# Layer norm over a matmul on one core: the opening worked on five row tiles with three quarters put aside, instead of seven with one

## The chip, the cores and the metric

The kernel runs on one core of one Trainium2 chip. The metric is the time of one execution on the device in microseconds (us), lower is better. The kernel before takes 249.03 us (median of three runs, 248.82 to 249.81).

The engines are named as in the profile: PE is TensorE, which multiplies and also transposes; PEld is its loading of weights; DVE is VectorE, ACT is ScalarE, POOL is GpSimd, and SP is SyncE, which here only issues DMA transfers. Each engine works through its own instructions in order and waits on semaphores for the others.

## The reference

```
x = np.matmul(a, b)                      # a, b: 2048 x 2048, float32
mean = np.mean(x, axis=-1, keepdims=True)
var = np.var(x, axis=-1, keepdims=True)
normalized = (x - mean) / np.sqrt(var + eps)
return (gamma * normalized + beta).astype(np.float32)
```

A row of the result can only be normalized when all its 2048 columns are there.

## The kernel before

**Tiling.** The rows of `a` form 16 row tiles of 128. The inner dimension forms 16 k tiles of 128, and four of them make a chunk (`KC`). The columns of `b` form four quarters of 512 (`NB`). One accumulator is one quarter of one row tile, 128 x 512 in float32. It fills one of eight PSUM banks and takes 16 matmuls, one per k tile, so there are 16 x 4 x 16 = 1024 matmuls (`mm`, L86). PSUM banks come from one pool of eight (L57), which the transposes use as well.

**Input.** All of `b` is brought to SBUF once, as float16 (`b16`). A piece of it lands in float32 in a staging buffer (the pool `stg` has six, each of 128 x 1024) and DVE casts it. `load_b1` brings one k tile of a quarter (256 KB), `load_b2` two k tiles (512 KB). PE needs `a` transposed. For the row tiles of the opening, `load_a1` and `load_a2` bring pieces of one chunk for one or two row tiles, DVE casts them, PE transposes them in `turn` (four 128 x 128 transposes per row tile and chunk, L239), and ACT copies the result to SBUF (L241). For the other row tiles, POOL issues a DMA that brings and casts a whole row tile (L339), and SP issues a DMA that transposes it (`turn_ahead`, L406). The POOL instruction at L290 copies one column of the last piece of `b`, so that the POOL transfers start only after it.

**The opening.** The first `R` = 7 row tiles are worked on together, because each piece of `b` that lands then feeds seven matmuls per k tile.

1. The first chunk of quarter 0. The pieces of `a` and `b` come in turn (list `arrivals`, L164): a0 b0 a1 b1 a2 b2 a3 b3 a4 a5 a6. PE multiplies what is there; where it would wait, matmuls on zeros are put in (`filler`, L232). The seven part sums over k tiles 0 to 3 are put aside by ACT in the SBUF tiles `x` (L297).
2. Quarter 1 over all 16 k tiles, in the order k tile by k tile, with the transposes of the later chunks in between (L300 to L315).
3. The other 12 k tiles of quarter 0 (L318 to L328). DVE adds what had been put aside (L325) and takes the batch statistics (L327).
4. Quarters 2 and 3 of these row tiles, one row tile after the other, three of them by quarter (`n_first`), the others by row.

Other accumulators are brought to SBUF by ACT and their statistics taken by DVE (`evacuate`, L96 and L97).

**After the opening** each row tile takes its four quarters in turn. `stats` joins the statistics, and `queue_norm` puts two pieces of normalization (two quarters each) into a list, from which `drain` takes one after a quarter; each piece ends in a store by SP. The transfers of the transposed row tile are issued four row tiles ahead (`turn_ahead(i + 4)`, L418). The last row tile has an ending of its own (`finish_row`).

**Order.** There is no scheduler: `manual_schedule` keeps each engine's instructions in the order in which the code emits them. A load function emits its DMA on SP and its cast on DVE, so where `bring` is called in between, the cast stands in DVE's queue at that place. A DMA into a staging buffer waits until DVE has cast what was in it.

Of the kernel before, what the change touches and what calls it, by code (L numbers as in the profile page):

```python
# [16 lines left out]
def kernel(  # L17
# [9 lines left out]
    nc = tc.nc  # L27
# [9 lines left out]
    KC = 4  # L37
    KW = KC * P
    n_kc = n_kt // KC
    R = 7  # L40
    early, e_cap, p_cap = 4, 3, 7
    n_first = 3
    assert n_kt % KC == 0 and n_nb == 4 and R % 2 == 1 and n_mt > R > n_first

    if isinstance(eps, bass.AP):
        eps_ap, eps_val = eps, None
# [36 lines left out]
    def mm(i, q, kt, first, last):  # L83
        if (i, q) not in acc:
            acc[i, q] = bank(f"acc{i}_{q}")
        nc.tensor.matmul(  # L86
            acc[i, q], at(i)[:, kt, :], b16[:, kt, ds(q * NB, NB)],
            start=first, stop=last,
        )
# [95 lines left out]
    def load_a1(i, c):  # L185
        st = half_stage()
        nc.sync.dma_start(st, a[ts(i, P), ts(c, KW)])  # L187
        a16_room(i, c)
        nc.vector.tensor_copy(a16_of[i, c], st)  # L189
# [9 lines left out]
    def load_b1(k):  # L199
        st = half_stage()  # L200
        nc.sync.dma_start(st, b[ts(k, P), 0:NB])  # L201
        nc.vector.tensor_copy(b16[:, k, 0:NB], st)  # L202

    def load_b2(k, q):
        st = stg.tile([P, 2, NB], FP32, tag="st", name=f"stb{q}_{k}")
        nc.sync.dma_start(
            st, b[ds(k * P, 2 * P), ds(q * NB, NB)].rearrange("(t p) n -> p t n", p=P))
        nc.vector.tensor_copy(b16[:, k:k + 2, ds(q * NB, NB)], st)  # L208
        return st
# [3 lines left out]
    def load_pair(j, c):  # L213
        if len(pairs[j]) == 2:
            load_a2(pairs[j][0], c)
        else:
            load_a1(pairs[j][0], c)

    for what in arrivals:
        (load_a1(what[1], 0) if what[0] == "a" else load_b1(what[1]))  # L220
    for c in range(n_kc):
        for h in (0, 1):
            load_b2(c * KC + 2 * h, 1)
            if c + 1 < n_kc:
                load_pair(2 * h, c + 1)
                load_pair(2 * h + 1, c + 1)

    warm = bank("warm")

    def filler(n, to=None):  # L230
        for _ in range(n):
            nc.tensor.matmul(warm if to is None else to, zeros[:, 0:P], zeros, start=True, stop=True)  # L232

    def turn(rows, c):
        n = len(rows)
        t_ps = psum.tile([P, n, KC, P], FP16, tag="ps", name=f"tps{rows[0]}_{c}")
        for m, i in enumerate(rows):
            for j in range(KC):
                nc.tensor.transpose(t_ps[:, m, j, :], a16_of[i, c][:, ts(j, P)], ident)  # L239
# [4 lines left out]
    queue, own = [], []  # L244
    turned, landed = set(), set()

    def emit(n):
        for _ in range(min(n, len(queue))):
            i, kt = queue.pop(0)
            done[i] += 1  # L250
            mm(i, 0, kt, done[i] == 1, done[i] == KC)

    done = [0] * R
    gaps = {0: (9, 3), 1: (1, 2), 2: (1, 2), 3: (3, 1), 4: (3, 0)}
    for what in arrivals:
        if what[0] == "b":
            k = what[1]
            now = [(i, k) for i in sorted(turned)]
            new = {i for i, _ in own}
            queue += [x for x in now if x[0] not in new] + own  # L260
            queue += [x for x in now if x[0] in new]
            own = []
            landed.add(k)
            continue
        i = what[1]
        if i < early:
            queue += own
            own = []
            emit(len(queue))
        before, after = gaps.get(i, (0, 0))  # L270
        filler(before)
        turn([i], 0)
        filler(after)
        if i >= early:
            emit(e_cap)
        queue += own
        turned.add(i)
        own = [(i, k) for k in sorted(landed)]
    queue += own
    queue.sort()  # L280

    later = [(k, 0) for k in range(KC, n_kt, 2)]
    later += [(k, q) for q in range(2, n_nb) for k in range(0, n_kt, 2)]

    def bring(n):
        for _ in range(n):
            k, q = later.pop(0)
            st = load_b2(k, q)
            if not later:
                nc.gpsimd.tensor_copy(gate, st[:, 0, 0:1])  # L290


    for p in range(R):
        emit(KC - done[p])
        xs[p] = xpool.tile([P, N], FP32, tag="x", name=f"x{p}")
        bnst[p] = stat.tile([P, n_nb, 6], FP32, tag="bnst", name=f"bnst{p}")
        nc.scalar.copy(xs[p][:, 0:NB], acc.pop((p, 0)))  # L297


    spots = {(h, p): 2 * h + m for h in (0, 1) for m, p in enumerate((2, 5))}  # L300
# [10 lines left out]
    for p in range(R):  # L311
        for kt in range(n_kt - KC, n_kt):
            mm(p, 1, kt, False, kt == n_kt - 1)
        bring(1)
        evacuate(p, 1)  # L315


    bring(len(later) - 4)  # L318
    for kt in range(KC, n_kt - KC):
        for p in range(R):  # L320
            mm(p, 0, kt, kt == KC, False)
    for p in range(R):
        for kt in range(n_kt - KC, n_kt):
            mm(p, 0, kt, False, kt == n_kt - 1)
        nc.vector.tensor_tensor(  # L325
            xs[p][:, 0:NB], acc[p, 0], xs[p][:, 0:NB], AluOp.add)
        nc.vector.bn_stats(bnst[p][:, 0, :], xs[p][:, 0:NB])  # L327
        bring(min(1, len(later)))  # L328
# [64 lines left out]
    def quarter(i, q):  # L393
        for kt in range(n_kt):
            mm(i, q, kt, kt == 0, kt == n_kt - 1)
# [9 lines left out]
                new_pair(t // 2)  # L405
            nc.sync.dma_start_transpose(at(t), a16[t])  # L406
# [59 lines left out]
```

## Time and profile before

| what | value |
|---|---|
| runs shown | 248.82, 249.03, 249.81 us |
| the profiled execution's own time | 249.5 us |
| its span, first to last instruction | 247.7 us |
| mean granted PE clock over the span | 0.989 |
| PE busy | 240.7 us (97%) |
| DVE busy | 173.0 us (70%) |
| ACT busy | 56.9 us (23%) |
| DMA read and written | 35.67 and 16.78 MB |

The durations below come from the profiled execution. Its own time is 1.8 us more than its span, and 0.5 us more than the median of the runs. In the profile, "L86" is line 86 of the kernel, and an entry such as "acc<-b,at 128x512 x1024" gives what is written and read, its shape and the number of instructions. Busy times of matmuls overlap, so that their mean duration (379 ns for those of L86) is longer than the step from one to the next.

### The profile page before, as it was taken

The numbers are of one execution on the slowest core, as the hardware profiler recorded it, in microseconds if no ns is written. First come the engines' busy times: TensorE is split into PE (matmuls) and PEld (weight loads), VectorE is DVE, ScalarE is ACT, GpSimd is POOL, SyncE is SP. The second block draws the span as 40 slices with busy tenths as digits, with TensorE's granted clock in tenths as the row PEclk, the third lists the DMA queues.
The fourth block names the chain that finished last, engine by engine and source line by source line (L and its number), as shares of the span: only waits on it lengthen the run. The fifth ranks groups of instructions, "written<-read, shape, count | busy, mean of one in ns | idle before, by whom it ended". The sixth has DMA issues, their size and how long they took to land.

```text
span 247.7 us, 3055 instructions
## 1 busy us (share of the span) xinstructions
PE 240.7 (97%) x1175; PEld 110.5 (45%) x1175; DVE 173.0 (70%) x307; ACT 56.9 (23%) x101; POOL 5.6 (2%) x15
## 2 busy tenths in 40 slices
PE   8999999999999999999999999999999999999983
PEld 3445555444444444444444444444444444444430
DVE  1454555965799999999999492856658292947873
ACT  2276446400013312221112121212111121112100
POOL 0000000000030000000000000000000000000000
PEclk9999999999999999999999999999999999999995
DMA  5999999999999239999999979180903122120404
GB/s 147 331 390 385 379 363 389 387 386 385 390 350 210 99 128 221 201 281 252 120 285 324 252 186 266 68 219 3 253 1 125 47 85 85 67 102 3 171 0 169
DMA packets 37846, 52.64 MB, mean 213 GB/s; under 512 B 20292, under 2 KB 20292, under 8 KB 37576
## 3 DMA queue, kind: packets, MB, share of 16 engines
q1 hardware_dynamic: 36536, 47.73, 58.1%
q0 software_dynamic: 1296, 4.72, 12.0%
q8 instruction: 9, 0.15, 0.2%
q14 instruction: 5, 0.04, 0.1%
HBM read 35.67 MB, written 16.78 MB: 212 GB/s over the span
## 4 chain that ended last, share of the span: by engine, by line
PE 92%; DMA 3%; SPq 2%; DVE 1%; issue 0%; ACT 0%
PE acc L86 88%; DMA st<-in_a_dram 3%; PE tps L239 2%; PE w L379 1%; SPq L187 1%; SPq L201 1%; DVE x L389 0%; DVE bnst L363 0%; DVE x L366 0%; DVE a16s L189 0%; PE nm_ps L374 0%; DVE mv L103 0%; ACT lead L375 0%; DVE nm L371 0%; DVE ve L105 0%
## 5 line engine op out<-in xcount | busy, mean ns | idle before, releaser
L86 PE MATMUL acc<-b,at 128*128 128x512 f16 x1024 | 224.1, 379 | 0.0
L86 PEld LDWEIGHTS <-at 128*128 128x128 f16 x1024 | 99.5, 98 | 117.8 <-ACT at L241 1.1
L97 DVE BATCH_NORM_STATS2 bnst<-x 128x6 f32<-128x512 f32 x56 | 38.4, 687 | 36.7 <-ACT x L96 36.7
L96 ACT COPY x<-acc 128x512 f32<-128x512 f32 x56 | 32.7, 585 | 129.5 <-PE acc L86 129.4
L118 DVE SCALAR_TENSOR_TENSOR x<-x,rstd,beta_b 128x512 f32<-128x512 f32 x61 | 43.1, 748 | 0.5
L112 DVE SCALAR_TENSOR_TENSOR x<-x,mv,gamma_b 128x512 f32<-128x512 f32 x60 | 42.1, 744 | 0.0
L208 DVE CAST b<-stb 128x1024 f16<-128x1024 f32 x30 | 20.8, 692 | 14.9 <-DMA stb<-in_b_dram 14.5
L241 ACT COPY at<-tps 128x512 f16<-128x512 f16 (+1 forms) x19 | 15.0, 787 | 21.2 <-PE tps L239 21.2
L232 PE MATMUL warm<-zeros 128*128 128x512 f16 x33 | 11.0, 466 | 1.2 <-DVE zeros L153 1.2
L197 DVE CAST a16s<-sta 128x1024 f16<-128x1024 f32 x9 | 6.2, 694 | 6.1 <-DMA sta<-in_a_dram 6.1
L107 ACT ACTIVATE sq<-ve 128x1 f32<-128x1 f32 x16 | 3.2, 203 | 31.3 <-DVE ve L105 31.3
L239 PEld LDWEIGHTS <-a16s 128*128 128x128 f16 x112 | 7.6, 99 | 6.2 <-DVE a16s L189 2.9
L239 PE MATMUL tps<-ident,a16s 128*128 128x128 f16 x112 | 9.6, 222 | 0.6 <-DVE a16s L189 0.5
L189 DVE CAST a16s<-st 128x512 f16<-128x512 f32 x10 | 4.3, 425 | 6.3 <-DMA st<-in_a_dram 6.3
L339 POOL DMA_DIRECT2D a<-in_a_dram x9 | 4.9, 547 | 70.0 <-DMA at<-a 69.7
L232 PEld LDWEIGHTS <-zeros 128*128 128x128 f16 x33 | 3.5, 114 | 5.3 <-issue 2.4
L327 DVE BATCH_NORM_STATS2 bnst<-x 128x6 f32<-128x512 f32 x7 | 4.9, 695 | 0.2
L325 DVE TENSOR_TENSOR x<-acc,x 128x512 f32<-128x512 f32 x7 | 4.8, 681 | 0.0
L103 DVE BATCH_NORM_AGGREGATE mv<-bnst 128x2 f32<-128x24 f32 x16 | 4.2, 264 | 0.5
L297 ACT COPY x<-acc 128x512 f32<-128x512 f32 x7 | 3.5, 632 | 0.0
L202 DVE CAST b<-st 128x512 f16<-128x512 f32 x4 | 1.7, 428 | 2.3 <-DMA st<-in_b_dram 2.3
L105 DVE TENSOR_TENSOR ve<-mv,eps_t 128x1 f32<-128x1 f32 x16 | 2.6, 160 | 0.5
(26 smaller groups left out, 17.4 us busy)
## 6 DMA issues: line engine op xcount, KB each, us to landing
stb<-in_b_dram SPq DMA_DIRECT2D x30, 512.0 KB, 7.4
out_dram<-x SPq DMA_DIRECT2D x30, 512.0 KB, 3.0
sta<-in_a_dram SPq DMA_DIRECT2D x9, 512.0 KB, 7.5
a<-in_a_dram POOLq DMA_DIRECT2D x9, 512.0 KB, 8.0
st<-in_a_dram SPq DMA_DIRECT2D x10, 256.0 KB, 7.0
st<-in_b_dram SPq DMA_DIRECT2D x4, 256.0 KB, 5.8
gamma_b<-in_gamma_dram SPq DMA_DIRECT2D x1, 1024.0 KB, 9.4
beta_b<-in_beta_dram SPq DMA_DIRECT2D x1, 1024.0 KB, 11.3
```

Of the source, the lines that this page charges most:

```text
L86: nc.tensor.matmul(acc[i, q], at(i)[:, kt, :], b16[:, kt, ds(q * NB, NB)], start=first, stop=last,)
L96: nc.scalar.copy(xs[i][:, qs], acc[i, q])
L97: nc.vector.bn_stats(bnst[i][:, q, :], xs[i][:, qs])
L112: nc.vector.scalar_tensor_tensor(xs[i][:, qs], xs[i][:, qs], mv[:, 0:1], gamma_b[:, qs], AluOp.subtract, AluOp.mult)
L118: nc.vector.scalar_tensor_tensor(xs[i][:, qs], xs[i][:, qs], rstd, beta_b[:, qs], AluOp.mult, AluOp.add)
L197: nc.vector.tensor_copy(held["a"][:, ds(i % KC, 2), :], st)
L208: nc.vector.tensor_copy(b16[:, k:k + 2, ds(q * NB, NB)], st)
L232: nc.tensor.matmul(warm if to is None else to, zeros[:, 0:P], zeros, start=True, stop=True)
L239: nc.tensor.transpose(t_ps[:, m, j, :], a16_of[i, c][:, ts(j, P)], ident)
L241: nc.scalar.copy(pair[i0 // 2][:, ds(i0 % 2, n), ds(c * KC, KC), :], t_ps)
L327: nc.vector.bn_stats(bnst[p][:, 0, :], xs[p][:, 0:NB])
L339: nc.gpsimd.dma_start(a16[i], a[ts(i, P), :])
```

## The change

The opening works on five row tiles (`R` = 5) instead of seven.

- The first chunk's pieces come in the order a0 b0 a1 a2 a3 a4 b1 b2 b3.
- Over k tiles 0 to 3, three quarters (0, 1 and 2, the list `ASIDE`) are multiplied and put aside in `x`, 15 part sums in all. Quarter 3 (`MAIN`) is the one that follows over all 16 k tiles. The pieces of `b` for k tiles 0 to 3 of quarters 1 and 2 come before the second chunk of `a`.
- Then the other 12 k tiles of quarters 0, 1 and 2 follow, each ending in an addition by DVE.
- Row tiles 5 and 6 are now brought by POOL and transposed by DMA like the later ones. The transposing transfers of row tiles 5 and 6 are issued ahead of the last part of the opening, those of the others two row tiles ahead instead of four.
- The pieces of normalization of the first five row tiles are all put into the list, and are taken from it from row tile 5 on.
- The fillers of the opening are 19 instead of 25, at other places.

```diff
-    R = 7
-    early, e_cap, p_cap = 4, 3, 7
-    n_first = 3
+    R = 5
+    ASIDE, MAIN = (0, 1, 2), 3
...
-    arrivals = []
-    for i in range(KC):
-        arrivals += [("a", i), ("b", i)]
-    arrivals += [("a", i) for i in range(KC, R)]
+    arrivals = [("a", 0), ("b", 0)] + [("a", i) for i in range(1, R)]
+    arrivals += [("b", k) for k in range(1, KC)]
...
+    for q in ASIDE[1:]:
+        load_b2(0, q)
+        load_b2(2, q)
+    load_pair(0, 1)
     for c in range(n_kc):
-        for h in (0, 1):
-            load_b2(c * KC + 2 * h, 1)
-            if c + 1 < n_kc:
-                load_pair(2 * h, c + 1)
-                load_pair(2 * h + 1, c + 1)
+        load_b2(c * KC, MAIN)
+        if c + 1 < n_kc:
+            if c > 0:
+                load_pair(0, c + 1)
+            load_pair(1, c + 1)
+        load_b2(c * KC + 2, MAIN)
+        if c + 1 < n_kc:
+            load_pair(2, c + 1)
...
+    later = [(k, q) for q in ASIDE for k in range(0 if q == MAIN else KC, n_kt, 2)]
...
+    def put_aside(p, q):
...
+        nc.scalar.copy(xs[p][:, ds(q * NB, NB)], acc.pop((p, q)))
+
+    def add_rest(p, q):
+        qs = ds(q * NB, NB)
+        nc.vector.tensor_tensor(xs[p][:, qs], acc[p, q], xs[p][:, qs], AluOp.add)
+        nc.vector.bn_stats(bnst[p][:, q, :], xs[p][:, qs])
+
+    filler(9)
+    turn([0], 0)
+    filler(3)
+    mm(0, 0, 0, True, False)
+    filler(1)
+    turn([1], 0)
+    filler(1)
+    for i in range(2, R):
+        filler(1)
+        turn([i], 0)
+        mm(i - 1, 0, 0, True, False)
+    mm(R - 1, 0, 0, True, False)
+    for kt in range(1, KC):
+        filler(2 if kt == 1 else 0)
+        for p in range(R):
+            mm(p, 0, kt, False, kt == KC - 1)
+            if kt == KC - 1:
+                put_aside(p, 0)
+
+    for q in ASIDE[1:]:
+        for p in range(R):
+            for kt in (0, 1):
+                mm(p, q, kt, kt == 0, False)
+        for p in range(R):
+            for kt in range(2, KC):
+                mm(p, q, kt, False, kt == KC - 1)
+            put_aside(p, q)
+
+    spots = {(0, 4): 0, (1, 1): 1, (1, 4): 2}
     for h in (0, 1):
         for p in range(R):
             for kt in (2 * h, 2 * h + 1):
-                mm(p, 1, kt, kt == 0, False)
+                mm(p, MAIN, kt, kt == 0, False)
             if (h, p) in spots:
                 turn(pairs[spots[h, p]], 1)
     for kt in range(KC, n_kt - KC):
         for p in range(R):
-            mm(p, 1, kt, False, False)
-        turn(pairs[kt % KC], kt // KC + 1)
+            mm(p, MAIN, kt, False, False)
+        if kt % KC > 0:
+            turn(pairs[kt % KC - 1], kt // KC + 1)
...
+    for p, n in enumerate((0, 1, 0, 1, 1)):
         for kt in range(n_kt - KC, n_kt):
+            mm(p, MAIN, kt, False, kt == n_kt - 1)
+        bring(n)
+        evacuate(p, MAIN)
+
+    for q, k_row, ahead, asked in (
+            (0, n_kt - KC, 7, (0, 0, 1, 0, 1)), (1, 2 * KC, 2, (0, 1, 1, 1, 1))):
+        bring(ahead)
+        for kt in range(KC, k_row):
+            for p in range(R):
+                mm(p, q, kt, kt == KC, False)
+        for p in range(R):
+            for kt in range(k_row, n_kt):
+                mm(p, q, kt, False, kt == n_kt - 1)
+            bring(asked[p])
+            add_rest(p, q)
...
-    for q in (2, 3):
-        for i in range(n_first):
-            quarter(i, q)
-            evacuate(i, q)
-            if q == 3:
-                close(i)
-    for i in range(n_first, n_mt):
+    turn_ahead(R)
+    turn_ahead(R + 1)
+    for p in range(R):
+        for kt in range(KC, n_kt):
+            mm(p, ASIDE[2], kt, kt == KC, kt == n_kt - 1)
+        add_rest(p, ASIDE[2])
+        queue_norm(p, *stats(p))
+    for i in range(R, n_mt):
         last = i == n_mt - 1
-        turn_ahead(i + 4)
-        for q in range(2 if i < R else 0, n_nb):
+        turn_ahead(i + 2)
+        for q in range(n_nb):
             quarter(i, q)
```

The other functions, `finish_row` among them, are the same.

More of the change, by code (lines that the diff above doesn't have):

```diff
@@ L39 @@
     n_kc = n_kt // KC
-    R = 7
-    early, e_cap, p_cap = 4, 3, 7
-    n_first = 3
-    assert n_kt % KC == 0 and n_nb == 4 and R % 2 == 1 and n_mt > R > n_first
+    R = 5
+    ASIDE, MAIN = (0, 1, 2), 3
+    assert n_kt % KC == 0 and n_nb == 4 and n_mt > R + 2
     if isinstance(eps, bass.AP):
@@ L242, in turn @@
             pair[i0 // 2][:, ds(i0 % 2, n), ds(c * KC, KC), :], t_ps)
[L244 to L283, printed above, removed]
+    later = [(k, q) for q in ASIDE for k in range(0 if q == MAIN else KC, n_kt, 2)]
     def bring(n):
@@ L290, in bring @@
                 nc.gpsimd.tensor_copy(gate, st[:, 0, 0:1])
[L293 to L300, printed above, removed]
+    def put_aside(p, q):
+        if xs[p] is None:
+            xs[p] = xpool.tile([P, N], FP32, tag="x", name=f"x{p}")
+            bnst[p] = stat.tile([P, n_nb, 6], FP32, tag="bnst", name=f"bnst{p}")
+        nc.scalar.copy(xs[p][:, ds(q * NB, NB)], acc.pop((p, q)))
[30 more added lines that the diff above has]
+    spots = {(0, 4): 0, (1, 1): 1, (1, 4): 2}
     for h in (0, 1):
@@ L308 @@
         for p in range(R):
-            mm(p, 1, kt, False, False)
-        turn(pairs[kt % KC], kt // KC + 1)
-    for p in range(R):
+            mm(p, MAIN, kt, False, False)
+        if kt % KC > 0:
+            turn(pairs[kt % KC - 1], kt // KC + 1)
+    for p, n in enumerate((0, 1, 0, 1, 1)):
         for kt in range(n_kt - KC, n_kt):
[L313 to L319, printed above, removed]
-        for p in range(R):
[L321 to L328, printed above, removed]
+            mm(p, MAIN, kt, False, kt == n_kt - 1)
[7 more added lines that the diff above has]
+                mm(p, q, kt, kt == KC, False)
+        for p in range(R):
+            for kt in range(k_row, n_kt):
+                mm(p, q, kt, False, kt == n_kt - 1)
+            bring(asked[p])
+            add_rest(p, q)
+    assert not later
     nc.sync.dma_start(gamma_b, gamma.unsqueeze(0).to_broadcast([P, N]))
```

## The prediction

> **What bounds the kernel now.** I read the page first: busy times, the chain that ended last, the groups of instructions.
>
> ```profile
> span 247.7 us, 3055 instructions
> PE 240.7 (97%) x1175; PEld 110.5 (45%) x1175; DVE 173.0 (70%) x307; ACT 56.9 (23%) x101; POOL 5.6 (2%) x15
> ...
> PE 92%; DMA 3%; SPq 2%; DVE 1%; issue 0%; ACT 0%
> ...
> L86 PE MATMUL acc<-b,at 128*128 128x512 f16 x1024 | 224.1, 379 | 0.0
> ...
> L232 PE MATMUL warm<-zeros 128*128 128x512 f16 x33 | 11.0, 466 | 1.2 <-DVE zeros L153 1.2
> ...
> L239 PE MATMUL tps<-ident,a16s 128*128 128x128 f16 x112 | 9.6, 222 | 0.6 <-DVE a16s L189 0.5
> ```
>
> PE is the bound, and 92% of the chain is its own work. What can change the time is what PE does, and the first microseconds, where it is fed by DMA. So next I read PE's timeline (start, duration, line).
>
> ```profile
> 11.74 1.03 PE L232 MATMUL warm<-zeros 128*128 128x512 f16 x4
> 13.23 0.40 PE L239 MATMUL tps<-ident,a16s 128*128 128x128 f16 x4 [0.46 <-DVE a16s L189]
> 13.46 0.81 PE L86 MATMUL acc<-b,at 128*128 128x512 f16 x3
> ...
> 39.10 1.67 PE L86 MATMUL acc<-b,at 128*128 128x512 f16 x7
> 40.61 0.39 PE L239 MATMUL tps<-ident,a16s 128*128 128x128 f16 x4
> 40.83 1.46 PE L86 MATMUL acc<-b,at 128*128 128x512 f16 x6
> ```
>
> The wait at 13.23 is the last that PE has before the last row's ending. From there to the statistics of the last accumulator (DVE L363, start 237.87) all is PE's own pace: in the chain, 912 matmuls take 196.85 us from 40.99, 0.2158 each, and eight transposes 0.45, 0.056 each. Up to 13.23 PE has done nine matmuls of the result (rows of L86 with x1, x3 and x5 before it) and 16 transposes. Check: 1015 x 0.2158 + 96 x 0.056 = 224.4; 13.2 + 224.4 = 237.7, and DVE starts 0.2 later.
>
> Third, DVE's timeline: each cast follows the landing of a piece.
>
> ```profile
> 11.01 0.43 DVE L189 CAST a16s<-st 128x512 f16<-128x512 f32 x1 [1.38 <-DMA st<-in_a_dram]
> 12.12 0.43 DVE L202 CAST b<-st 128x512 f16<-128x512 f32 x1 [0.68 <-DMA st<-in_b_dram]
> 12.75 0.43 DVE L189 CAST a16s<-st 128x512 f16<-128x512 f32 x1 [0.20 <-DMA st<-in_a_dram]
> ...
> 14.06 0.43 DVE L189 CAST a16s<-st 128x512 f16<-128x512 f32 x1 [0.23 <-DMA st<-in_a_dram]
> 15.41 0.69 DVE L208 CAST b<-stb 128x1024 f16<-128x1024 f32 x1 [0.92 <-DMA stb<-in_b_dram]
> ...
> 36.50 0.69 DVE L197 CAST a16s<-sta 128x1024 f16<-128x1024 f32 x1 [0.76 <-DMA sta<-in_a_dram]
> ...
> 39.79 0.69 DVE L208 CAST b<-stb 128x1024 f16<-128x1024 f32 x1 [0.65 <-DMA stb<-in_b_dram]
> ```
>
> The first nine are those of pieces of 256 KB, cast at 4.62, 6.22, 6.92, 7.58, 8.60, 9.21, 11.01, 12.12 and 12.75. Then 512 KB come each 1.35 to 1.4 us, without a gap: the stream is full (377 to 381 GB/s, below). I take it that a piece's time depends on its place in the stream, not on whether it is of a or b, since all are 128 rows of 2 KB.
>
> ```profile
> 6.20:13.20 7.00, 6.42 (x36) 2.50 (x34) 3.42 (x8) 1.89 (x4) 0.00 (x0) 1.00 1.02 334
> 13.20:41.00 27.80, 27.77 (x200) 15.55 (x201) 13.66 (x22) 15.46 (x21) 0.00 (x0) 1.00 1.04 381
> ```
>
> (Windows: length, busy PE, PEld, DVE, ACT, POOL, then granted clock, DMA share, GB/s.)
>
> **Part 1: fewer transposes on PE.** Row tiles 5 and 6 leave the opening: 5 x 16 = 80 transposes instead of 112. Of the 32 that go, all but what lay in the waiting before 13.23 is on the path (counted in part 2). With them go two casts of L189 (0.425) and three of L197 (0.694) on DVE, 2.9 us, and 4.3 us of copies on ACT; DVE gets eight additions more (15 instead of 7, 0.681 each), 5.4 us. Neither engine sets PE's time there, so I cost these at nothing: ACT's cover is the free banks (8 less 5 accumulators), DVE's is checked in part 4. ACT's copies of accumulators stay 63.
>
> **Part 2: the first chunk.** With the casts' times above, 0.43 for a cast and 0.6 for ACT's copy of a transposed tile: a1 to a4 are there at 7.4, 8.0, 9.0 and 9.6; PE transposes each (0.22), multiplies each with b0, and is through with five matmuls and 20 transposes at about 11.0. Two fillers lead to 11.45, when b1 (seventh piece) is cast. Five matmuls (1.08) end at 12.53; b2 is cast at 12.55, and five more end at 13.63; b3 has come at 13.18, so the last five end at 14.71. The next piece is 512 KB (k tiles 0 and 1 of quarter 1); it ends where the eleventh small piece ended, 14.06, and is cast at 14.75. Three further ones of b follow each 1.35, each good for ten matmuls (2.16). From 14.7 on PE has work. It then has 1024 - 20 = 1004 matmuls and 80 - 20 = 60 transposes left: 216.7 + 3.3 = 220.0, and the end comes at 234.7 + 0.2 = 234.9, against 237.87: **-2.9**. Of this, 1.6 is transposes (28 fewer left at 14.7, when before has 24 behind it) and 1.3 six matmuls done earlier.
>
> **Part 3: the stream over quarter 3.** Before, the cast at 39.79 is of the piece with which 14 x 256 KB + 17 x 512 KB = 12 MB have come. In the new order the last piece of quarter 3 (k tiles 14, 15) is also reached with 12 x 256 + 18 x 512 KB = 12 MB, so it is cast at 40.5. PE: quarters 1 and 2, 40 matmuls, to 23.4; quarter 3 with its transposes (k tiles 0 to 3, 20 matmuls and 20 transposes) to 28.9; eight k tiles of 1.08 with 40 transposes to 39.7; k tile 14 is wanted at 40.2. The piece of k tiles 10, 11 (10.75 MB, where the cast at 36.50 stands) is ready at 37.2 and wanted at 36.95. So PE, which is early now, meets the stream: a wait of about 0.3 in all, **+0.3**. Before it had 0.8 to spare at k tile 14. If the stream is as much faster as the spread of steps allows (1.35 for all) it is 0; if it is 4% slower over these 27 us, 1.4.
>
> The page "DMA: Bandwidth & Descriptors" of the Trainium skill, section Specifications, gives a limit of about 358 GB/s per core for HBM, which speaks against an order that puts PE earlier on the same stream. By it the 25.7 us from 14.06 to 39.8 would be 1.6 longer, and the sum -1.0 instead of -2.6. The row has 381 GB/s, and I go by the row.
>
> **Part 4: DVE and the banks after that.** An addition with its statistics and a cast in between step 1.92 apart in the rows of L325 (65.69, 67.61, 69.53). In the rest of quarter 1 a row tile's eight matmuls take 1.73, so DVE falls behind by about 0.2 each; behind each addition stands a cast that PE wants. The tightest is the last piece of quarter 2: cast at about 71.5, wanted at 72.5. Nothing, with 1 us of cover; without it, up to 1 (five triples begun one cast later). Banks: the fourth accumulator of a quarter needs the first addition of the one before, done 2 us ahead.
>
> **Part 5: row tiles 5 and 6 by POOL and SP.** Two transfers more on POOL (11), two transposing ones more on SP (11). Their chain, in the rows of before:
>
> ```profile
> 70.46 0.18 POOL L290 COPY gate<-stb 128x1 f32<-128x1 f32 x1 [68.89 <-DMA stb<-in_b_dram]
> 71.02 1.73 POOL L339 DMA_DIRECT2D a<-in_a_dram  x3 [0.37 <-DVE bnst L327]
> ...
> 91.81 3.27 SPq L406 DMA_TRANSPOSE at<-a  x1
> ...
> DMA to landing us min/median/max: 4.9/7.4/10.8
> ...
> DMA to landing us min/median/max: 4.9/5.0/10.6
> ```
>
> (The last lines: landing of the transfers of a, and of the transposing ones.) Now row tile 5 is wanted at 14.7 + 300 x 0.2158 + 3.3 + 0.3 = 83.0, where row tile 7 was wanted at about 113. The last piece of b goes into the buffer of the piece cast between the additions of quarter 0, at about 60.8, and lands at 65 to 66; then POOL (0.6), the transfer (6.7 for the first of three before), the transposition (5.0 undisturbed): 78 to 79. Nothing, with 4 to 5 us to spare. With the slow ends of both rows it is 66 + 0.6 + 10.8 + 10.6 = 88, a wait of 5. I take the near rows; the slow transposition ran beside another transfer, and so could this one. On SP nothing but the transpositions of 6 and 7 and stores is behind the wait.
>
> Later, transpositions are issued two row tiles ahead, behind two stores that wait for DVE: one quarter costs DVE 3.3 to 3.9 (bn, centre, scale: rows from 94.52 to 101.71), so four cost 13.9 beside 13.8 of PE, and the lag stays near 4. 27.6 ahead, less 4 and about 4 of the work, leaves some 20 for a landing of at most 10.6. The list of ten pieces shrinks by two per row tile, to one by row tile 9, so the last row's ending is the same. Nothing.
>
> **Sum.** -2.9 + 0.3 = -2.6 on a span of 247.7, so 245.1. The profiled execution itself is 249.5, 0.5 above the median of the runs; I take the change off the median: 249.03 - 2.6 = **246.4**.
>
> **The rivals.**
> B, the stream holds PE longer: parts 3 and 4 at their other ends, 1.4 instead of 0.3, gives 247.5. For it: PE has no slack left there. Against: the steps are even.
> C, the clock. Fillers before 5.2 us step about 0.42 apart (nine in 4.02), twice the later pace, so a cold PE costs double. PE is busy 6.42 of 7.00 us in the second window; in the new order I count some 5.3 of 7. If it fell back for the first chunk, 15 matmuls cost 0.21 more each, 3.2, less what the stream hides: up to 249.6. Against: no gap over 0.5 us. The page "TensorE: Matmul & The Clock Gate", Part 1, asks for an idle window of about 3.4 us before the rate is halved. By it this rival costs nothing.
> D, the other side: row tile 5 is late. Part 5 at its slow ends: 246.4 + 5 = 251.4. It decides against the change from a landing 2.6 us behind the want, at 85.6. For it: the chain of transfers has 4 to 5 us to spare where before it had 16 (91.8 + 5.0 against 113). Against: its middle rows end at 79.
> That the change does nothing is excluded by the instruction counts; 32 transposes are gone from PE's queue.
>
> **How the numbers follow.** Changes under 0.5% (1.2 us) can't be told from none here. Forecast 0.58 (its own range 245.8 to 247.0: wait 0 to 0.9); B 0.16, still faster by 0.6%; D 0.15, about half of it within 0.5% and half slower; C 0.05, mostly within; 0.06 for what I don't see, taken as slower. Faster 0.74, same 0.11, slower 0.15. Forecast and B hold 0.74; the range goes a little below the forecast, and up into D and C to 249.2.
>
> **What would show it.** 80 transposes; PE without a wait from about 14.7, but with short ones by DVE's casts near 37 and 40; 1.3 us of PE's work earlier at 14.7; the first L85 matmul of row tile 5 at 83 with no wait; the last row's statistics at about 235.3. A wait of PE on the transposing DMA near 83 shows D; matmuls stepping 0.42 after 7 us show C; waits of over 1 us between 25 and 45, or at 70 to 73, show B. The prediction is wrong if the small pieces land otherwise in the new order, above all the first of 512 KB.

## The result, and the profile after

The changed kernel takes 247.01 us (median of four runs, 246.63 to 247.19), the kernel before 249.25 us (median of four). The ratio is 0.9918, with a 95% interval of 0.9899 to 0.9936. It is faster by 2.2 us; 246.4 had been forecast. The profiled execution is the fastest of the four, with 246.63 us and a span of 244.6.

From the page of the changed kernel: span, busy times, the chain that ended last, the matmuls and the transposes.

```profile
span 244.6 us, 2975 instructions
PE 236.8 (97%) x1137; PEld 108.0 (44%) x1137; DVE 175.2 (72%) x310; ACT 52.6 (21%) x96; POOL 7.2 (3%) x17
...
PE 94%; DMA 2%; DVE 1%; ACT 0%; SPq 0%; issue 0%
...
L85 PE MATMUL acc<-b,at 128*128 128x512 f16 x1024 | 223.5, 379 | 0.7 <-DVE b L199 0.4
...
L243 PE MATMUL tps<-ident,a16s 128*128 128x128 f16 x80 | 6.8, 219 | 0.4 <-DVE a16s L186 0.3
```

PE is still the bound, and 32 transposes are gone from it. The timelines of PE and of DVE in the changed kernel (start, duration, line):

```profile
10.91 0.39 PE L85 MATMUL acc<-b,at 128*128 128x512 f16 x1 [0.28 <-ACT at L245]
11.14 0.59 PE L236 MATMUL warm<-zeros 128*128 128x512 f16 x2
11.57 14.19 PE L85 MATMUL acc<-b,at 128*128 128x512 f16 x65
...
39.52 0.39 PE L243 MATMUL tps<-ident,a16s 128*128 128x128 f16 x4
39.74 10.52 PE L85 MATMUL acc<-b,at 128*128 128x512 f16 x48
```

```profile
6.47 0.43 DVE L199 CAST b<-st 128x512 f16<-128x512 f32 x1 [1.05 <-DMA st<-in_b_dram]
...
9.89 0.43 DVE L199 CAST b<-st 128x512 f16<-128x512 f32 x1 [0.26 <-DMA st<-in_b_dram]
10.56 0.43 DVE L199 CAST b<-st 128x512 f16<-128x512 f32 x1 [0.24 <-DMA st<-in_b_dram]
11.24 0.43 DVE L199 CAST b<-st 128x512 f16<-128x512 f32 x1 [0.25 <-DMA st<-in_b_dram]
12.59 0.69 DVE L205 CAST b<-stb 128x1024 f16<-128x1024 f32 x1 [0.93 <-DMA stb<-in_b_dram]
...
38.74 0.69 DVE L205 CAST b<-stb 128x1024 f16<-128x1024 f32 x1 [0.66 <-DMA stb<-in_b_dram]
```

From 11.57 on PE has no wait: it then has 1019 matmuls and 60 transposes to do, 1019 x 0.2158 + 60 x 0.056 = 223.3, which ends at 234.9. DVE begins the statistics of the last accumulator at 235.06, where it was 237.87 before: 2.8 us earlier. First the line of the kernel before, then that of the changed kernel:

```profile
237.87 0.70 DVE L363 BATCH_NORM_STATS2 bnst<-acc 128x6 f32<-128x512 f32 x1 [1.41 <-PE acc L86]
...
235.06 0.70 DVE L364 BATCH_NORM_STATS2 bnst<-acc 128x6 f32<-128x512 f32 x1 [1.42 <-PE acc L85]
```

Of the 2.8, 2.0 come from 36 transposes fewer behind that point (60 where there were 96) and 1.7 from the earlier start, less 0.9 for four matmuls more. The last row's ending is 0.3 shorter in this execution, which makes the 3.1 us between the two spans.

The pieces do not land as in the kernel before. From the second on they come at an even step of 0.67 us, and the ninth is cast at 11.24 instead of 12.75. The windows of the changed kernel (length, busy PE, PEld, DVE, ACT, POOL, granted clock, DMA share, GB/s) show the fuller stream, 396 GB/s where it was 334:

```profile
6.20:13.20 7.00, 6.16 (x38) 2.78 (x37) 4.02 (x9) 2.64 (x5) 0.00 (x0) 1.00 1.05 396
13.20:41.00 27.80, 27.80 (x175) 14.29 (x173) 13.17 (x21) 15.65 (x25) 0.00 (x0) 1.00 1.05 387
```

The chain of transfers for row tile 5, from the timelines of POOL and SP; the last line is the landing of the first of the three transposing transfers, counted from its issue:

```profile
65.05 0.26 POOL L255 COPY gate<-stb 128x1 f32<-128x1 f32 x1 [63.48 <-DMA stb<-in_b_dram]
65.60 2.23 POOL L340 DMA_DIRECT2D a<-in_a_dram  x3 [0.30 <-DVE b L205]
81.12 0.53 POOL L340 DMA_DIRECT2D a<-in_a_dram  x1 [13.29 <-DMA at<-a]
...
73.72 14.34 SPq L407 DMA_TRANSPOSE at<-a  x3
...
DMA to landing us min/median/max: 6.9/6.9/6.9
```

The transposition of row tile 5 is issued at 73.72 and lands 6.9 later, at 80.6 (POOL goes on at 81.12, when the buffer is free). By its step PE begins row tile 5 at 11.57 + 315 x 0.2158 + 3.4 = 82.9. There were two us to spare.

### The profile page after: what moved, and what is told of

It is laid out like the page before. It is cut to its first block, busy times and chain, and to the rows that moved or that the text cites. A ratio compares the mean times of both kernels' runs of the same rounds, so it can differ in the third digit from the quotient of the medians.

```text
span 244.6 us, 2975 instructions
## 1 busy us (share of the span) xinstructions
PE 236.8 (97%) x1137; PEld 108.0 (44%) x1137; DVE 175.2 (72%) x310; ACT 52.6 (21%) x96; POOL 7.2 (3%) x17
## 4 chain that ended last, share of the span: by engine, by line
PE 94%; DMA 2%; DVE 1%; ACT 0%; SPq 0%; issue 0%
PE acc L85 90%; DMA st<-in_a_dram 2%; PE tps L243 2%; PE w L380 1%; PE warm L236 1%; DVE x L390 0%; DVE bnst L364 0%; DVE x L367 0%; ACT at L245 0%; DVE a16s L186 0%; SPq L198 0%; PE nm_ps L375 0%; SPq L184 0%; DVE mv L102 0%; ACT lead L376 0%
## 5 line engine op out<-in xcount | busy, mean ns | idle before, releaser
L205 DVE CAST b<-stb 128x1024 f16<-128x1024 f32 x30 | 20.4, 687 | 13.0 <-DMA stb<-in_b_dram 12.9
L245 ACT COPY at<-tps 128x512 f16<-128x512 f16 (+1 forms) x14 | 10.8, 768 | 14.1 <-PE tps L243 14.0
L265 DVE TENSOR_TENSOR x<-acc,x 128x512 f32<-128x512 f32 x15 | 10.3, 686 | 3.0 <-PE acc L85 2.7
L236 PE MATMUL warm<-zeros 128*128 128x512 f16 x27 | 9.0, 463 | 1.2 <-DVE zeros L152 1.2
L340 POOL DMA_DIRECT2D a<-in_a_dram x11 | 6.4, 587 | 91.6 <-DMA at<-a 91.3
L243 PEld LDWEIGHTS <-a16s 128*128 128x128 f16 x80 | 5.4, 98 | 4.7 <-DVE a16s L186 2.4
L243 PE MATMUL tps<-ident,a16s 128*128 128x128 f16 x80 | 6.8, 219 | 0.4 <-DVE a16s L186 0.3
L194 DVE CAST a16s<-sta 128x1024 f16<-128x1024 f32 x6 | 4.2, 694 | 4.0 <-DMA sta<-in_a_dram 4.0
L186 DVE CAST a16s<-st 128x512 f16<-128x512 f32 x8 | 3.4, 427 | 5.0 <-DMA st<-in_a_dram 4.8
L236 PEld LDWEIGHTS <-zeros 128*128 128x128 f16 x27 | 2.9, 113 | 4.6 <-issue 2.2
## 6 DMA issues: line engine op xcount, KB each, us to landing
beta_b<-in_beta_dram SPq DMA_DIRECT2D x1, 1024.0 KB, 10.3
```

The costliest lines, as they stand in the source:

```text
L245: nc.scalar.copy(pair[i0 // 2][:, ds(i0 % 2, n), ds(c * KC, KC), :], t_ps)
L265: nc.vector.tensor_tensor(xs[p][:, qs], acc[p, q], xs[p][:, qs], AluOp.add)
```

## The experiments

The time at which the first piece of b lands differs from execution to execution, and everything behind moves with it. So the table gives for each profiled execution the start of that piece's cast, the start of the statistics of the last accumulator, and the difference of the two, beside the median time and the ratio to the kernel before on the same chip.

| kernel | first cast of b | last statistics | difference | median, us | ratio, 95% interval |
|---|---|---|---|---|---|
| before | 6.22 | 237.87 | 231.65 | 249.25 | |
| changed | 6.47 | 235.06 | 228.59 | 247.01 | 0.9918, 0.9899 to 0.9936 |
| changed, once more | 6.64 | 235.21 | 228.57 | 247.09 | 0.9923, 0.9897 to 0.9948 |
| e1, pieces in turn | 6.38 | 237.99 | 231.61 | 250.99 | 1.0090, 1.0057 to 1.0123 |
| e4, one quarter aside | 6.79 | 237.84 | 231.05 | 249.90 | 1.0031, 1.0014 to 1.0049 |
| e3, transposes twice | 7.11 | 239.05 | 231.94 | 250.71 | 1.0068, 1.0044 to 1.0091 |
| e7, seven row tiles, a first | 6.66 | 238.49 | 231.83 | 250.03 | 1.0032, 1.0018 to 1.0046 |
| e5, row tile 5 later | 6.73 | 235.47 | 228.74 | 248.18 | 0.9959, 0.9940 to 0.9978 |
| f3, row tile 5 third | 7.24 | 250.87 | 243.63 | 260.95 | 1.0478, 1.0449 to 1.0506 |
| e2, no fillers | 6.60 | 234.64 | 228.04 | 246.28 | 0.9890, 0.9865 to 0.9915 |
| f2, no fillers, again | 7.08 | 235.83 | 228.75 | 247.57 | 0.9925, 0.9903 to 0.9946 |
| e6, three moves | 6.84 | 234.99 | 228.15 | 246.88 | 0.9906, 0.9889 to 0.9922 |
| f1, two moves | 6.98 | 234.59 | 227.61 | 246.59 | 0.9895, 0.9870 to 0.9921 |
| g1, two moves, fillers kept | 7.12 | 234.80 | 227.68 | 246.65 | 0.9891, 0.9874 to 0.9909 |

### The changed kernel once more

> The changed kernel once more, as the measure for the runs beside it. If the even landing of the first nine pieces (a step of 0.67 us, the ninth cast at 11.2) belongs to the kernel and not to one execution, it shows again; the statistics of the last accumulator start at 235.1. If it is chance, the ninth cast moves by a microsecond or more.

The ninth piece is cast at 11.38, with the same step of 0.67. The even landing belongs to the kernel, and the difference in the table repeats to 0.02 us.

### e1: the pieces of the first chunk in turn

```diff
-    arrivals = [("a", 0), ("b", 0)] + [("a", i) for i in range(1, R)]
-    arrivals += [("b", k) for k in range(1, KC)]
+    arrivals = []
+    for i in range(KC):
+        arrivals += [("a", i), ("b", i)]
+    arrivals += [("a", i) for i in range(KC, R)]
```

> The changed kernel with the first chunk's pieces in turn (a0 b0 a1 b1 a2 b2 a3 b3 a4), PE's order unchanged. Theory (a piece's time goes by its place in the stream, and the order decides what PE finds): a4 is the ninth piece, cast at 11.2 if the stream stays even, or at 12.8 as in the kernel before; then transposition, ACT's copy, a matmul and two fillers, so that the second k tile starts at 13.2 or 14.7 instead of 11.6: 1.6 to 3.1 us longer. Rival (the gain is the transposes alone, the order of the pieces is worth nothing): no change. A gap of over 1 us ahead of the seventh piece would say that the alternation makes it.

The kernel is slower than the one before. DVE's timeline and then PE's in this run:

```profile
9.11 0.43 DVE L201 CAST b<-st 128x512 f16<-128x512 f32 x1 [0.27 <-DMA st<-in_b_dram]
9.91 0.43 DVE L188 CAST a16s<-st 128x512 f16<-128x512 f32 x1 [0.37 <-DMA st<-in_a_dram]
10.98 0.43 DVE L201 CAST b<-st 128x512 f16<-128x512 f32 x1 [0.64 <-DMA st<-in_b_dram]
12.28 0.43 DVE L188 CAST a16s<-st 128x512 f16<-128x512 f32 x1 [0.88 <-DMA st<-in_a_dram]
```

```profile
12.77 0.40 PE L245 MATMUL tps<-ident,a16s 128*128 128x128 f16 x4 [1.54 <-DVE a16s L188]
...
14.50 14.19 PE L85 MATMUL acc<-b,at 128*128 128x512 f16 x65
```

The last piece of a comes ninth and PE, whose order is unchanged, waits for it: the same run of 65 matmuls starts at 14.50 instead of 11.57, and the difference in the table grows by 3.0, within what was expected. So the order of the pieces carries the gain of this kernel, and the transposes alone don't. (An order of PE's work made for five row tiles with the pieces in turn was not run.) The steps are uneven again (0.80, 1.07, 1.30), though the gap ahead of the seventh piece was not over 1 us; which pieces come late is another than before. The ten times spread from 249.56 to 254.18 (the table's row leaves out the two longest, 253.64 and 254.18), with a mean granted clock of 0.993 in the fastest execution and 0.979 to 0.986 in those above 250.5. Only the fastest has a profile, and in it the clock was 1.00 through the opening. That the clock fell in the opening of the others, as f2 shows it below, fits these figures and is not shown.

### e7: the new order alone, in the kernel before

```diff
-    arrivals = []
-    for i in range(KC):
-        arrivals += [("a", i), ("b", i)]
-    arrivals += [("a", i) for i in range(KC, R)]
+    arrivals = [("a", 0), ("b", 0)] + [("a", i) for i in range(1, R)]
+    arrivals += [("b", k) for k in range(1, KC)]
```

> The kernel before (seven row tiles, one quarter put aside) with the first chunk's pieces in the new order alone: a0 b0 a1 to a6 b1 b2 b3. Theory on the landing (pieces of a and b in turn land unevenly and late, those of a in a row evenly): a step of 0.67 us up to the eleventh, cast at 12.6 instead of 14.1. Then PE works without a wait from 13.1 with 28 transposes and 7 to 9 matmuls behind it, 0.7 to 0.9 us less in all, 248.2. Rival (the uneven landing is of eleven small pieces, or chance): gaps of over 1 us again, and a time from 0.3 less to 0.7 more.

The landing is as expected, the time is not. DVE's timeline (the eleventh piece) and PE's:

```profile
12.77 0.43 DVE L200 CAST b<-st 128x512 f16<-128x512 f32 x1 [0.25 <-DMA st<-in_b_dram]
```

```profile
12.82 0.38 PE L86 MATMUL acc<-b,at 128*128 128x512 f16 x1
13.04 0.39 PE L237 MATMUL tps<-ident,a16s 128*128 128x128 f16 x4
13.44 6.65 PE L86 MATMUL acc<-b,at 128*128 128x512 f16 x30
```

Eleven small pieces land evenly, the last 1.3 us earlier than in the kernel before. But PE has only four matmuls behind it at 13.44, where it had nine at 13.23 before: with only one piece of b among the first eight there was nothing to multiply, and it did fillers. Twelve transposes more are behind it (0.7), five matmuls fewer (1.1), and with 0.2 of later start that is 0.6, the difference between the two last statistics (238.49 and 237.87); by the table's difference it is 0.2, since the first piece of b came 0.4 later, and by the ratio of the times 0.3%. I had counted seven to nine matmuls at that point. The order by itself makes the seven tile opening slower; it pays with five row tiles, of which all are transposed by 10.3 us, so that each piece of b finds five matmuls.

### e4: five row tiles, one quarter put aside

```diff
-    ASIDE, MAIN = (0, 1, 2), 3
+    ASIDE, MAIN = (0,), 3
...
-    later = [(k, q) for q in ASIDE for k in range(0 if q == MAIN else KC, n_kt, 2)]
+    later = [(k, q) for q in range(3) for k in range(0 if q else KC, n_kt, 2)]
...
-            add_rest(p, q)
+            (add_rest if q == 0 else evacuate)(p, q)
...
-        for kt in range(KC, n_kt):
-            mm(p, ASIDE[2], kt, kt == KC, kt == n_kt - 1)
-        add_rest(p, ASIDE[2])
+        for kt in range(n_kt):
+            mm(p, 2, kt, kt == 0, kt == n_kt - 1)
+        evacuate(p, 2)
```

(Quarter 1's k loop also starts at 0, with six pieces instead of two brought ahead of it.)

> Five row tiles, but only quarter 0 put aside; quarters 1 and 2 are worked over all 16 k tiles after quarter 0, with the same number of matmuls and transposes as in the changed kernel. Theory (the quarters put aside are the work that covers the stream): the last piece of quarter 3 comes 2 MB earlier, ready at 34.0, but PE wants it at 31.5, having 40 matmuls less to do by then: waits of about 2.5 us in all between 15 and 34 us, the end 2.5 us later, so that nothing of the gain is left. Rival (five row tiles with fewer transposes are enough): no change.

PE's timeline in this run has the waits:

```profile
24.84 1.24 PE L85 MATMUL acc<-b,at 128*128 128x512 f16 x5 [1.53 <-DVE b L205]
...
30.94 1.24 PE L85 MATMUL acc<-b,at 128*128 128x512 f16 x5 [0.50 <-DVE b L205]
```

The difference in the table grows by 2.5, as expected, of which 2.0 are in these two waits. By the times all of the gain is lost (0.6 of it is left by the table's difference), with the same number of transposes as in the changed kernel. The 40 matmuls of quarters 1 and 2 over k tiles 0 to 3 are the work that covers the stream.

### e3: the transposes of three chunks done twice

```diff
-                nc.tensor.transpose(t_ps[:, m, j, :], a16_of[i, c][:, ts(j, P)], ident)
+                for _ in range(2 if c else 1):
+                    nc.tensor.transpose(t_ps[:, m, j, :], a16_of[i, c][:, ts(j, P)], ident)
```

> The changed kernel with each of the 60 transposes of the second to fourth chunk done twice (the second writes the same values again). Theory (PE is the bound in the opening, so each transpose costs its own step there): 60 x 0.056 = 3.3 us longer, the statistics of the last accumulator at 238.4, a time of 250.4. Rival (the stream of pieces or DVE binds in that stretch, and PE has room): less than 1 us.

PE's first transposes of the second chunk, sixteen in the place of eight (25.60 0.61 in the changed kernel):

```profile
26.25 1.06 PE L244 MATMUL tps<-ident,a16s 128*128 128x128 f16 x16
```

The difference grows by 3.4 (231.94 against 228.58), 0.056 for each of 60. In that stretch a transpose costs its own step, so the 28 fewer that were left for it are worth 1.6 us.

### e5 and f3: row tile 5 late

e5 brings row tile 5 last of the first three that POOL fetches, and transposes 6 ahead of it:

```diff
-    for i in range(R, n_mt):
+    for i in [R + 2, R + 1, R] + list(range(R + 3, n_mt)):
...
-    turn_ahead(R)
     turn_ahead(R + 1)
+    turn_ahead(R)
```

> The changed kernel with row tile 5 brought last instead of first of the three that POOL fetches at 65.6, and transposed after row tile 6. Theory (the price of a late row tile 5 is one for one behind the time at which PE wants it, 82.7; it is there at about 81.1 in the changed kernel): its transfer lands at about 78, its transposition 7 to 10 us later, 85 to 88, so PE waits 2.5 to 5.5 us in front of row tile 5, and the end moves by that: 249.6 to 252.6. Rival (there are 4 to 5 us to spare, as the prediction has it): a wait of at most 1 to 3 us. If nothing moves, that chain is not near the path.

The transpositions were issued from 75.66 on, and the second landed at 83.8 or a little earlier, not at 85 to 88: the two took 5.2 and 4.4 from issue to landing, not 7 to 10. PEld's timeline shows what was left of the wait:

```profile
83.31 4.65 PEld L85 LDWEIGHTS <-at 128*128 128x128 f16 x23 [0.48 <-DMA at<-a]
```

In the profiled execution PE itself lost 0.2 by it; in the others the median is 1.1 us above that of the changed kernel. Less than expected by the theory, and inside what the rival allows, so this run tells only that the chain is within some 2 us of PE's want. f3 makes it later, by the order 6, 7, 5 of the transposing transfers:

```diff
-    turn_ahead(R)
     turn_ahead(R + 1)
+    turn_ahead(R + 2)
+    turn_ahead(R)
...
-        turn_ahead(i + 2)
+        if i > R:
+            turn_ahead(i + 2)
```

> The changed kernel with the transposing transfers in the order row tile 6, 7, 5. Theory (a late row tile 5 costs PE one for one): the third transposing transfer landed 15.9 after its issue at 80.7 in the changed kernel, at 96.6, and row tile 5 is wanted at 82.7: PE waits 8 to 14 us in front of row tile 5, and the end moves by as much, 255 to 261. PE then stands idle for more than 3.4 us: if the clock falls after such an idle time, as the page TensorE: Matmul & The Clock Gate of the Trainium skill has it, the first matmuls after it step 0.42 for some microseconds, 1 to 2 us more; if not, they step 0.216 at once. Rival (later work makes up for the wait): less than half of the wait at the end.

PE's timeline and windows of this run:

```profile
96.73 13.59 PE L85 MATMUL acc<-b,at 128*128 128x512 f16 x53 [12.92 <-DMA at<-a]
```

```profile
84.00:88.00 4.00, 0.00 (x0) 0.00 (x0) 1.66 (x4) 0.20 (x1) 0.70 (x2) 0.89 1.00 145
88.00:96.00 8.00, 0.00 (x0) 0.00 (x0) 0.00 (x0) 0.00 (x0) 0.00 (x0) 0.50 1.09 145
96.00:100.00 4.00, 3.27 (x8) 1.19 (x9) 0.00 (x0) 0.00 (x0) 0.53 (x1) 0.50 0.45 57
100.00:102.00 2.00, 2.00 (x9) 0.83 (x8) 0.00 (x0) 0.00 (x0) 0.00 (x0) 0.81 0.86 172
102.00:104.00 2.00, 2.00 (x11) 0.94 (x10) 1.01 (x2) 0.59 (x1) 0.00 (x0) 1.00 0.00 0
```

The wait is 12.9, and the difference in the table grows by 15.1. (This execution was the slowest of its four; the median is 13.9 above that of the changed kernel.) The other 2.1 are the clock. It falls to 0.50 some 3.3 us after PE has stopped (a mean of 0.89 over 84 to 88) and is back at 100.8 (0.81 over 100 to 102), so PE works at half its pace for 4.0 us, which costs 2.0. Nothing later makes up for a wait here. The page "TensorE: Matmul & The Clock Gate", Part 1, gives half the rate after an idle window of about 3.4 us and the full rate after about as much sustained work; this run has 3.3 and 4.0.

### e2 and f2: no fillers behind the first matmul

```diff
-    filler(1)
     turn([1], 0)
-    filler(1)
     for i in range(2, R):
-        filler(1)
         turn([i], 0)
...
-        filler(2 if kt == 1 else 0)
```

> The changed kernel without the seven fillers behind the first matmul. Theory (PE's own chain transposition, ACT copy, matmul and the fillers set the start of the second k tile, not the stream): it starts at 10.9 instead of 11.6, and all ends 0.6 us earlier, since the piece wanted at k tile 14 of quarter 3 was 0.7 early. Rival 1 (the clock falls without the fillers): matmuls step 0.42 for a while, 1 to 3 us longer. Rival 2 (the stream binds next): the start moves by 0.6, but a wait of about as much appears near 40 us, and the end stays.

```profile
10.86 14.42 PE L85 MATMUL acc<-b,at 128*128 128x512 f16 x66 [0.30 <-ACT at L245]
```

In this run 1020 matmuls are left at 10.86 (1019 at 11.57 in the changed kernel), and the difference in the table is 0.5 smaller; the time was 246.28, and the four executions lie within 0.2 us. The start of the second k tile was set by PE's own work, not by the stream. Beside the next kernel it ran again, on another chip:

> The changed kernel without the seven fillers, once more, as the measure for the run beside it. As before: 246.3, the statistics of the last accumulator at 234.6.

It took 247.57 this time, from 246.31 to 247.97, no better than with the fillers. The windows of its profiled execution show why:

```profile
7.00:8.00 1.00, 0.38 (x1) 0.00 (x0) 0.64 (x2) 0.00 (x0) 0.00 (x0) 1.00 1.05 404
8.00:9.00 1.00, 0.67 (x5) 0.41 (x6) 0.64 (x2) 0.09 (x1) 0.00 (x0) 0.64 1.04 402
9.00:10.00 1.00, 0.99 (x6) 0.49 (x7) 0.62 (x2) 0.92 (x2) 0.00 (x0) 0.50 1.06 406
10.00:11.00 1.00, 1.00 (x8) 0.72 (x7) 0.66 (x2) 0.54 (x2) 0.00 (x0) 0.50 1.06 352
11.00:12.00 1.00, 0.85 (x6) 0.28 (x3) 0.62 (x2) 0.73 (x2) 0.00 (x0) 0.65 1.02 375
```

The first piece of b came at 7.08, PE waited 1.0 us for it and less for others, and the granted clock fell to 0.50 from 8.3 to 11.7. Its last statistics start 1.2 later than in e2: 0.5 is the later first piece, 0.7 the clock (the difference in the table). The six executions have a mean clock of 0.994 (at 246.31 us) or 0.982 to 0.987 (from 247.28 up); only the one has a profile.

Do the fillers keep the clock up? In three profiled executions with fillers the first piece of b came as late (e3 7.11, g1 7.12, f3 7.24), and the granted clock was 1.00 from 5 to 13 us in all three; f3 ran on the chip of f2 and has the changed kernel's opening. That speaks for it. It is not settled, since without fillers e2 (first piece at 6.60) and f1 (6.98) kept their clock in the profiled executions, and the changed kernel itself did not run on f2's chip. The fillers look like lost time in an execution in which nothing goes wrong, and they are probably what keeps others from losing a microsecond.

### e6, f1 and g1: what is left in the first chunk

e6 adds three moves to e2: the fifth row tile's first matmul comes after four of the second k tile's; in the second and third chunk the second piece of quarter 3 comes ahead of the second pair of a; k tiles 12 and 13 of quarter 3 are worked k tile by k tile.

```diff
-    mm(R - 1, 0, 0, True, False)
     for kt in range(1, KC):
         for p in range(R):
+            if kt == 1 and p == R - 1:
+                mm(p, 0, 0, True, False)
             mm(p, 0, kt, False, kt == KC - 1)
...
-            if c > 0:
-                load_pair(0, c + 1)
-            load_pair(1, c + 1)
+            load_pair(0 if c > 0 else 1, c + 1)
         load_b2(c * KC + 2, MAIN)
         if c + 1 < n_kc:
+            if c > 0:
+                load_pair(1, c + 1)
             load_pair(2, c + 1)
...
+    for kt in range(n_kt - KC, n_kt - 2):
+        for p in range(R):
+            mm(p, MAIN, kt, False, False)
     for p, n in enumerate((0, 1, 0, 1, 1)):
-        for kt in range(n_kt - KC, n_kt):
+        for kt in range(n_kt - 2, n_kt):
```

> The changed kernel without the seven fillers, and with three moves: the fifth row tile's first matmul after four of the second k tile's (PE waited 0.3 us there for ACT's copy); in the second and third chunk the second piece of quarter 3 ahead of the second pair of a; and k tiles 12 and 13 of quarter 3 worked k tile by k tile. Theory (PE's chain in the first chunk is the only thing left, and the moves keep the stream ahead): 0.4 us less than without the fillers alone, the statistics of the last accumulator at 234.2, a time of 245.8. Rival (the stream binds): PE waits near 36 or 40 us, and the end is at 234.5 or later.

It is at 228.15 in the table, 0.1 behind e2, and the time of 246.88 is 1.1 above what was expected. PE's timeline has a new wait, at the first cast of quarter 0's later pieces; DVE's two lines stand behind it:

```profile
43.86 46.48 PE L85 MATMUL acc<-b,at 128*128 128x512 f16 x214 [0.27 <-DVE b L205]
...
42.52 0.69 DVE L96 BATCH_NORM_STATS2 bnst<-x 128x6 f32<-128x512 f32 x1 [2.90 <-ACT x L95]
43.13 0.68 DVE L205 CAST b<-stb 128x1024 f16<-128x1024 f32 x1
```

That cast stands in DVE's queue behind the statistics of the first row tile, which come 1.5 us later than in e2 (42.52 against 41.01), since with the third move the first row tile's quarter ends later. f1 has the first two moves without it:

> Without the fillers, with two of the three moves alone: the fifth row tile's first matmul after four of the second k tile's, and in the second and third chunk the second piece of quarter 3 ahead of the second pair of a. Quarter 3's last four k tiles are worked row tile by row tile again. Theory (what the three moves together lost was lost by the third, which lets DVE's statistics come 2 us later, with the casts queued behind them, and so quarter 0, the additions and the banks): 0.4 us less than without the fillers alone, the statistics of the last accumulator at 234.2, a time of 245.9. Rival (the first chunk can't start earlier because the stream binds): a wait near 36 or 39.5, the same time as without the fillers alone.

At 227.61 it is 0.4 ahead of e2, as expected, and nothing waits near 36 or 39.5. But its six times lie at 245.79 to 246.16 with a mean clock from 0.992, and at 247.02 to 247.59 with 0.984 to 0.989. What the slower three lost has no profile. g1 takes the same two moves, leaves out only the two fillers ahead of the second k tile, keeps the others, and has five instead of three where PE waits for the first piece of b:

> The changed kernel with the two moves (the fifth row tile's first matmul after four of the second k tile's; the second piece of quarter 3 ahead of the second pair of a in the second and third chunk), without the two fillers ahead of the second k tile, but with the other fillers kept and two more where PE waits for the first piece of b. Theory (fillers cost nothing where PE waits, keep the clock up there, and cost their step where it does not wait): the second k tile starts at about 10.5 with four matmuls behind it, against 11.6 with five, 0.9 us gained, of which the stream takes back up to 0.3; the clock stays at 1.00 from 7 us on in all executions; statistics of the last accumulator at 234.3 to 234.6, 246.2 to 246.4, in a spread as narrow as that of the changed kernel. Rival (PE's share of work ahead of 10 us is still too small): a spread up to 247.6, as without the fillers.

Its median is 246.65, and the six times lie between 246.34 and 246.97. PE's timeline has no wait between 8 and 14 us, and the difference in the table is 0.9 less than that of the changed kernel, as expected. The absolute times are not, since the first piece of b came late in this execution (7.12), and the last statistics stood at 234.80, beyond the 234.6 named. Against the kernel before it is faster by 1.1% (0.9891, to 0.9909); against the changed kernel by about 0.4 us, not measured side by side, and their intervals overlap.

## Why the prediction was right, point by point

**Transposes (part 1).** Confirmed: e3 has the price of one, 0.056, where it lies on the path, and the others' work stayed beside PE.

**The first chunk (part 2).** The end of this stretch was right, its reasons not, and that the number stood is in part luck. The step that failed is the one by which "a piece's time depends on its place in the stream, not on whether it is of a or b". The prediction itself names small pieces that land otherwise as its sign of being wrong, and they did: the later ones came evenly, the ninth 1.5 us earlier, the first of 512 KB cast at 12.59 instead of 14.06, and the first piece of b 0.1 to 1.0 later (6.47 to 7.24 in twelve executions with a ahead, 6.22 and 6.38 with the pieces in turn, which are too few to call this the order's doing). So the second k tile did not wait for b1, cast at 9.89; it began at 11.57, against 11.45 forecast, because PE had first to go through transposition, ACT's copy, the last matmul and two fillers. PE's chain hangs on a4, and there the late start and the even step nearly cancel: it was ready at 9.63, forecast was 9.6. That is the luck. The sum of -2.9 for parts 1 and 2 was measured as 2.8 between the last statistics of the two profiles.

**The stream (part 3).** The 0.3 was not there. The pieces kept most of their lead: the last piece of quarter 3 was cast at 38.74 instead of the 39.8 reckoned with, and PE wanted it 0.7 after it was ready. That PE is near the stream was right: with e4's order it waits 2.0. The skill's figure of 358 GB/s, which the prediction weighed from the page "DMA: Bandwidth & Descriptors", is contradicted again, by 387 and 396 GB/s in the windows.

**DVE and the banks (part 4).** Right in the step (1.92, the additions at 65.18, 67.10 and 69.02) and in that nothing waits. e6 shows, at another place (43.86), that a cast behind late statistics can hold PE.

**Row tile 5 (part 5).** The step "78 to 79 ... 4 to 5 us to spare" was mis-sized: it landed at 80.6 with 2 to spare. The transfer took 8.1 from issue to landing where the sum had 6.7, and the transposition 6.9 beside the other transfers instead of the undisturbed 5.0. The rival D was real in kind: one for one, and with the clock more (f3).

**The clock (rival C).** Right that it did not decide: the granted clock was 1.00 from 6.2 to 13.2. But I gave it 0.05 by counting PE's share of work and by the page's idle window of about 3.4 us, and f2 shows that an opening only a little emptier can fall into it with no wait of over 1.0 us. There the measurement goes against the rule of the page "TensorE: Matmul & The Clock Gate", Part 1. The changed kernel's fillers probably keep it out.

**The time.** 247.01 instead of 246.4. Of the 2.8 in the profiles, 2.2 are in the medians. The profiled execution had the earliest first piece of b of all those with a ahead, and was the fastest of its four runs; the forecast had that piece at 6.22 and no spread. What the other three executions lost was not seen, since they have no profile. The second profiled execution of the same kernel (247.36) shows that the first piece is not all of it: its last statistics are 0.15 later, and its last row's ending is 0.65 longer (the last four matmuls, L380, take 2.66 instead of 1.98, with a granted clock of 0.73 instead of 0.94 from 238 to 241).

## What to carry to other kernels

Read at which point the bound engine stops waiting and how much of its work is behind it then: the time is that point plus the rest at its own step, and that sum was within 0.3 us in the traces of the changed kernel and of e2. An order of arrivals is worth something only together with an order of work that can use each piece when it comes; the same order won 3.0 us in one opening and won nothing in another (e7). Before taking out fill work that seems to stand on the path, look at several executions: it may hold the clock for those whose first piece is late.

## What the runs showed of the hardware that was not expected

- Pieces of the same size and shape land evenly, 0.67 us apart, when those of a come in a row and then those of b (twelve executions, with five and with seven row tiles), and with gaps up to 1.8 us between casts when they alternate (two executions of two kernels); the DMA rate from 6.2 to 13.2 us was 396 in the changed kernel and 334 GB/s in the kernel before. The alternation alone does not make that gap: e1, with the pieces in turn, has 375, and those with a ahead 378 to 396. Why was not tested.
- The granted clock fell to 0.50 in f2 although PE never stopped for over 1.0 us at a time, with busy shares of 0.61, 0.54, 0.38 and 0.67 in the four microseconds from 5 to 9; f1 had 0.59, 0.45, 0.38 and 0.57 there and kept its clock in the profiled execution. So the share alone doesn't decide.
- Three transposing transfers in a row, beside others, landed 6.9, 4.4 and 15.9 us after their issue. The third took 13.4 to 15.9 in eleven executions and 6.8 in a twelfth (e3, which issued it 3.1 after the second, the others 1.9 to 2.4 after it). Why was not tested.
